# A two-layer decoder on one core: the result table's additions bound late in the last expert, pick matrices written by ScalarE, the table zeroed during attention, router bias and second tile reordered

## The chip, the cores and the metric

The kernel runs on one core of one Trainium2 chip. The metric is the device time of one execution in microseconds (us), as the median of several runs. Engines are named as in the profile: PE (TensorE matmul), PEld (its weight load), DVE (VectorE), ACT (ScalarE), POOL (GpSimd), SP (SyncE, which here only issues DMAs).

## The reference

A decoder of two layers on 256 tokens of width 1024, with 16 learned rows put in front (272 rows in all). Cut to what the change touches:

```python
for i in range(2):
    if i == 0: mix = rglru_block(h, ...)          # gated linear recurrence
    else:      mix = gla_block(h, ...)            # gated linear attention, 4 heads, chunks of 64
    h = layer_norm(ALPHA * h + mix, g, b)
    if i == 0: ff = swiglu(h, w_in, w_out)        # dense, width 3584
    else:      ff = moe_swiglu(h, ...)
    h = layer_norm(ALPHA * h + ff, g, b)

def moe_swiglu(h, router, w_in, w_out):           # 8 experts, 2 of them for each token
    logits = h @ router
    top_w, top_idx = softmax(top_k(logits, 2))
    y = 0
    for e in range(8):
        y = y + gate[:, e] * (silu(h @ w_in[e].gate) * (h @ w_in[e].up)) @ w_out[e]
    return y
```

## The kernel before

**Products and weights.** Every fp32 product is made of three fast ones: `mm3` (L271 to L275) multiplies the high part of a weight with the low part of the data, the low part with the high, and high with high. So each weight piece of 128x1024 has to be split before PE may use it: SP loads raw weights (L97), ACT casts a piece to its high part `whi` (L127), DVE subtracts to get the low part `wlo` (L137). Loads, casts and subtractions run ahead of PE by a few pieces.

**The mixture of experts.** The second half of the run goes through 8 experts of 7 stages each, 56 stages in all. A stage takes 12 weight pieces: 8 for the products `pg` and `pu` (tile xe of an expert's gathered tokens times the gate and up matrices), 4 for the product `y` back to width 1024. Between them ACT and DVE make `hb` = silu(pg) * pu (L1329, L1330), PE transposes it (`pt`), and ACT and DVE split that into `hh` and `hl` (L268, L269). The 56 `hb` rows mark the stages in what follows.

**Odd jobs.** All other work of this phase (slots of the experts, gathers, the table) is put into a queue `side`, whose `step` takes out some entries at each weight piece; an entry `lambda: None` is a blank that only lets time pass. The queue decides where the jobs stand in the program. A scheduler then sets the order of instructions on each engine from that program; `behind([x], f)` forbids that it places what f emits ahead of instruction x on the same engine. The part between attention and experts (from L1067) is in a section where the written order stands as it is.

**The result table.** Each of the first seven experts writes its result rows into a table `yd` in DRAM by an indirect DMA from POOL (`scatter`, L1371); rows that no expert writes must read as zero, so `clear` (L1272 to L1276) fills the table ahead of the first scatter. In the last expert `fetch_back` (L1282, POOL) reads the table back into two tiles `back`, and `add_back` (L1293, L1295) adds their four 128x1024 blocks on DVE to the residual `acc`. `split_acc` (L1446 on ACT, L1447 on DVE) splits the sum for a last matmul that adds it to the eighth expert's result.

**Slots.** For each expert, DVE writes selection matrices `sel` (L934) from the positions, PE multiplies them into `gs` (L1230), and DVE copies that to `slot_of` (L1232). `spread_pick` (L1199, POOL) makes four 128x512 matrices `pick`, which copy a row of a small table to all partitions by a matmul (`spread`).

**Router and second tile.** `router_sums` and `router_bias` (L707 to L712) give the bias of the router logits, from DVE's sums `rbs` by one matmul `rtb`. The 256 tokens are two tiles of 128. For each, `project` multiplies the attention result (`go`, `go11b`), `x3_add` adds it to the residual (L957), `x3_turn` transposes it on PE (`x3T`, L970), `logits` makes `lg`, `choose` finds the two experts (L1007 to L1013, `mask`), `rank` counts (L1020), `place` writes `pos` and `sel`. `x3_low` on POOL (L995) splits the normalised tile.

Of the kernel before, what the change touches and what calls it, by code (L numbers as in the profile page):

```python
# [11 lines left out]
F32 = mybir.dt.float32  # L12
# [57 lines left out]
class Weights:  # L70
# [62 lines left out]
    def lower(self, i, src, hi, lw):  # L133

        u, c, n = self.pieces[i]
        low = self.nc.gpsimd if i in self.aside else self.low
        low.tensor_sub(lw[:, :n], src, hi[:, :n])  # L137
        if c + n == self.units[u][1]:
            del self.raws[u]
            place = self.place.pop(u)  # L140
            if place[1] in self.retired:
                self.retired.pop(place[1])()
            else:
                self.free.append(place)
            self.load()
# [40 lines left out]
def trunk_kernel(ctx: ExitStack, tc: tile.TileContext, xT_d, rgp_d, lnT_d, rgin_d, rgg_d, rgout_d,  # L186
# [46 lines left out]

    const = ctx.enter_context(tc.tile_pool(name="const", bufs=1))
    ps = ctx.enter_context(tc.tile_pool(name="ps", bufs=8, space=PSUM))

    def bank(name):
        return ps.tile([P, 512], F32, tag="ps", name=name)
# [398 lines left out]
    wu = gp.tile([P, 512], F32, tag="vm", name="wu", bufs=1)  # L637
    nc.sync.dma_start(wu, wup_d)
    cm = gp.tile([P, P], F32, name="cm")
    cmask = gp.tile([P, P], U32, name="cmask")  # L640
    nc.gpsimd.affine_select(out=cm, in_=ones, pattern=[[1, P]], compare_op=ALU.is_ge, fill=0.0, base=0,
                            channel_multiplier=-1)
# [108 lines left out]

    side.drain()
    vm = gp.tile([P, D], F32, tag="vm", name="vm", bufs=1)
    side.put([lambda: None] * 36 + [router_sums] + [lambda: None] * 12 + [router_bias])
    for e in range(KD):
        pp = bank(f"vT{e}")
        for k in range(KD):
# [86 lines left out]
    def split_out(e):  # L844
        split(oh[:, e:e + 2], ol[:, e:e + 2], gr[:, e:e + 2])
# [25 lines left out]
    split_out(0)  # L871
    split_out(2)
    normalize(2)
    side.put([lambda: gate_out(4), lambda: gate_out(6), lambda: split_out(4), lambda: split_out(6)])
    pgo = [[bank(f"go{i}{q}") for q in range(2)] for i in range(2)]

    halves = [(slice(0, 256), pgo[1][1][:, :256]), (slice(256, 512), bank("go11b")[:, :256])]
# [40 lines left out]
    sels = {}  # L918
    late = ctx.enter_context(tc.tile_pool(name="late", bufs=1, reuse_waits="tile"))
    W.widen([(late, "late0"), (late, "late1"), (late, "late2"), (late, "xeC")])  # L920
    dram = ctx.enter_context(tc.tile_pool(name="dram", bufs=1, space=bass.MemoryType.DRAM))
    x3d = dram.tile([NX, D], F32, name="x3d")
    yd = dram.tile([2 * NX + P, D], F32, name="yd")
    gb = ctx.enter_context(tc.tile_pool(name="rows", bufs=1, reuse_waits="tile"))
    x3T = [gb.tile([P, 2, NX], F32, tag="xg", name=f"x3T{k2}", bufs=4) for k2 in range(4)]

# [140 lines left out]
    with tc.manual_schedule(engines={mybir.EngineType.PE, mybir.EngineType.DVE, mybir.EngineType.Activation}):  # L1067
        project((4, 5, 6, 7), ws, 0, 0)
        x3_add(0, 0)
        x3_stats(0, 0)  # L1070
        project((4, 5, 6, 7), ws, 0, 1)
        x3_turn(0, (0, 1))
        x3_add(0, 1)
        x3_stats(0, 1)
        project((4, 5), ws, 1, 0)
        x3_scale(0)
        x3_turn(0, (2, 3))
        logits(0, (0, 1))
        project((6,), ws, 1, 0)
        for q in range(2):  # L1080
            x3_norm(0, q)
        logits(0, (2, 3))
        project((7,), ws, 1, 0)
        choose(0)
        for q in range(2):
            x3_high(0, q)
            x3_low(0, q, nc.gpsimd)
        x3_add(1, 0)
        for k2 in range(2):
            x3_stats(1, k2)  # L1090
        project((4,), ws, 1, 1)
        project((5,), ws, 1, 1, halves[:1])
        x3_turn(1, (0, 1))
        project((6, 7), ws, 1, 1, halves[:1])
        pr = rank(0)
        x3_add(1, 1, halves[:1])
        W.later = []
        W.split_until(W.n_split + 1)
        place(0, pr)
        x3_stats(1, 2)  # L1100
        project((5,), ws, 1, 1, halves[1:])
        logits(1, (0, 1))
        x3_turn(1, (2,))
        project((6, 7), ws, 1, 1, halves[1:])
        x3_add(1, 1, halves[1:])
        W.split_until(W.n_split + 1)
        res.close()
        m2 = ctx.enter_context(tc.tile_pool(name="moe2", bufs=1, reuse_waits="tile"))
        W.widen([(m2, "xeB")])
        rows_of(0)  # L1110
        xgp[0] = bank("xg00")
        gather_part(xgp[0], 0, 0, 0)
        x3_turn(1, (3,))
        x3_stats(1, 3)
        x3_scale(1)
        logits(1, (2,))
        xgp[1] = bank("xg01")
        gather_part(xgp[1], 1, 0, 0)
        logits(1, (3,))
        for k2 in (2, 3):  # L1120
            xgp[k2] = bank(f"xg0{k2}")
            gather_part(xgp[k2], k2, 0, 0)
        choose(1)
        keep_warm(7)
        pr = rank(1)
        keep_warm(4)
        for q in range(2):
            x3_norm(1, q)
            x3_high(1, q)
        place(1, pr)  # L1130
        for q in range(2):
            x3_low(1, q, nc.vector)
        for k2s in ((0, 1), (2, 3)):
            for s in range(2):
                for k2 in k2s:
                    gather_part(xgp[k2], k2, 0, 1, (s,))
        first_rows(0, 0)
        lower(1)
        first_rows(1, 0)
        lower(1)  # L1140
        W.split_until(W.n_split + 1)
        first_rows(2, 0)
        lower(1)
        W.split_until(W.n_split + 1)
        first_rows(3, 0)
        lower(1)
        W.later = None
# [38 lines left out]

    picks, rows_hl = {}, []

    def spread_split():

        rows_hl.append(const.tile([P, 256], F32R, tag="onetri", name="rows_hl", bufs=1))
        nc.scalar.copy(rows_hl[0], rows)
        for at in (slice(32, 40), slice(96, 104)):
            nc.vector.tensor_sub(rows_hl[0][at], rows[at], rows_hl[0][at])

    def spread_pick(n, c):
        picks[n, c] = gb.tile([P, 4, P], F32R, tag="xg", name=f"pick{n}{c}", bufs=4)
        high, low = (ident[:, p0:p0 + 4, None].broadcast_to([P, 4, P]) for p0 in (64 * n + 4 * c, 64 * n + 4 * c + 32))
        nc.gpsimd.tensor_add(picks[n, c], high, low)  # L1199

    def spread(n, c, s):

# [65 lines left out]
            nc.tensor.transpose(pt[:, k * P:(k + 1) * P], x3r[e][:, (4 * h + k) * P:(4 * h + k + 1) * P], ident)  # L1268
        split(*(t[:, 4 * h:4 * h + 4].rearrange("p k t -> p (k t)") for t in xe[e]), pt)

    def clear():

        zero = late.tile([P, D], F32, tag="yrow", name="zero", bufs=1)
        nc.gpsimd.memset(zero, 0.0)
        for a in range(2 * NX // P):
            nc.gpsimd.dma_start(yd[a * P:(a + 1) * P], zero)  # L1276

    def store_x3():
        nc.gpsimd.dma_start(x3d.rearrange("(i p) d -> p i d", p=P), acc)

# [23 lines left out]
    def rows_1():  # L1304
        side.put([lambda: rows_of(1)] + [lambda k2=k2: split_rows(1, k2) for k2 in range(4)]
                 + [spread_split, lambda: behind(chosen, gate_values)]
                 + [lambda: [slots(e) for e in range(2)]])
        for e in range(2, NE, 2):
            side.put([lambda e=e: [pair(e)] + [select(g, i) for g in (e, e + 1) for i in range(2)],
                      lambda e=e: [slots(g) for g in (e, e + 1)]])  # L1310
        side.put([addresses, clear] + [lambda c=c: spread_pick(0, c) for c in range(2)]
                 + [lambda c=c, s=s, i=i: residual(c, s, i) for c in range(2) for s in range(2) for i in range(2)]
                 + [store_x3, lambda: None, lambda: fetch(2)])

# [143 lines left out]
    for n in range(NJ + 1):  # L1458
# [4 lines left out]
        if n > 0:  # L1463
            e, j = (n - 1) // JM, (n - 1) % JM
            if n == NJ:
                side.drain()
            stage_out(n - 1)
            if n == RB:
                W.retire("xeB", rows_1)
            if n == 5 * JM:  # L1470
                for tag in ("xeC", "late1", "late2"):
                    W.retire(tag, lambda: None)
            if j == 3 and 1 <= e < NE - 1:
                side.put([lambda e=e, h=h: turn(e + 1, h) for h in range(2)])
                if e < NE - 2:
                    side.put([lambda e=e: fetch(e + 2)])
            if e == NE - 1 and j == 0:
                lng[0] = m2.tile([P, 2, D], F32, tag="xeA", name="lng", bufs=1)
                side.put([last_slots] + [lambda c=c: spread_pick(1, c) for c in range(2)] + [lambda: None] * 4)
                side.put([lambda c=c, s=s: nc.scalar.copy(lng[0][:, c, s * 512:(s + 1) * 512], spread(1, c, s))  # L1480
                          for c in range(2) for s in range(2)])
                side.put([fetch_back] + [lambda: None] * 8)
                side.put([lambda k=k, i=i: add_back(k, i) for k in range(2) for i in range(2)])
                side.put([lambda i=i, s=s: split_acc(i, s) for s in range(2) for i in range(2)])
            if j == JM - 1 and e < NE - 1:
                while not placed:
                    side.items.popleft()()
                scatter(e)
# [163 lines left out]
```

## Time and profile before

| what | value |
|---|---|
| median of 3 runs | 1537.59 us (1536.28 to 1541.04) |
| profiled execution, own time | 1538.53 us |
| its span, first to last instruction | 1536.8 us |
| mean granted TensorE clock | 0.991 |
| PE busy | 1496.2 us (97%) |
| DVE busy | 1267.0 us (82%) |
| ACT busy | 1057.8 us (69%) |
| POOL busy | 125.6 us (8%) |

The span is what the trace covers; 1.7 us of the profiled execution's time lie outside it. The profiled execution took 0.94 us more than the median. The granted clock is TensorE's, as a share of full speed, and a busy share is an average over the whole span, so it says nothing of a single stage.

### The profile page before, as it was taken

What the parts mean: (1) busy time and instruction counts of PE and PEld (TensorE: products, weight loads), DVE (VectorE), ACT (ScalarE), POOL (GpSimd) and SP (SyncE); (2) the same over time, 40 slices, a digit from 0 to 9 for tenths busy, and PEclk for the clock granted to TensorE, in tenths of its full rate; (3) what the DMA queues carried; (4) which work ended last, traced back from release to release, by engine and by line L of the source; (5) the groups of instructions that cost most, each with busy time, mean ns of one, the idle gap of its engine ahead of it and who ended that gap; (6) DMA issues with size and microseconds to landing.
All of it is one profiled execution on the core that took longest, in us unless ns stands there. A gap on an engine that the chain in (4) does not pass through costs nothing.

```text
span 1536.8 us, 22261 instructions
## 1 busy us (share of the span) xinstructions
PE 1496.2 (97%) x8377; PEld 1305.5 (85%) x8377; DVE 1267.0 (82%) x1487; ACT 1057.8 (69%) x1364; POOL 125.6 (8%) x158
## 2 busy tenths in 40 slices
PE   8989999999999999999999999999999999997996
PEld 8989999999998878788888888888888888886884
DVE  7699755555876699899998889889899898896996
ACT  6866544444774598677887777677777786785774
POOL 5443000011100000200000000000000000000001
PEclk9999999999999999999999999999999999999998
DMA  9536544445452589899999999999998999998872
GB/s 369 182 134 220 192 172 171 144 172 187 165 189 86 220 314 391 307 341 423 400 371 369 360 380 387 364 391 383 359 390 309 368 372 389 377 361 341 308 269 104
DMA packets 68963, 450.65 MB, mean 293 GB/s; under 512 B 8144, under 2 KB 8432, under 8 KB 20720
## 3 DMA queue, kind: packets, MB, share of 16 engines
q1 hardware_dynamic: 65584, 437.10, 75.5%
q0 software_dynamic: 3264, 12.06, 2.0%
q8 instruction: 67, 1.10, 0.3%
q14 instruction: 48, 0.39, 0.1%
HBM read 441.26 MB, written 7.86 MB: 292 GB/s over the span
## 4 chain that ended last, share of the span: by engine, by line
PE 88%; DVE 6%; ACT 2%; issue 2%; DMA 1%; POOL 1%; SPq 0%; DVEq 0%; POOLq 0%; ACTq 0%
PE y L274 7%; PE y L275 7%; PE y L273 7%; PE pg L273 7%; PE pg L274 6%; PE pu L273 6%; PE pg L275 6%; PE pu L275 6%; PE pu L274 6%; DVE wlo L137 2%; PE fg L274 2%; PE fo L273 2%; PE fo L275 2%; PE fu L273 2%; PE fg L275 2%
## 5 line engine op out<-in xcount | busy, mean ns | idle before, releaser
L137 DVE TENSOR_TENSOR wlo<-raw,whi 128x1024 fp32r<-128x1024 f32 (+1 forms) x839 | 981.7, 1216 | 129.9 <-ACT whi L127 122.7
L127 ACT CAST whi<-raw 128x1024 fp32r<-128x1024 f32 (+1 forms) x841 | 835.1, 1037 | 169.6 <-PE fu L275 43.5
L274 PE MATMUL y<-wlo,hh 128*128 128x512 f32 x448 | 177.1, 395 | 9.5 <-DVE wlo L137 9.5
L273 PE MATMUL pg<-whi,xe 128*128 128x512 f32 x448 | 178.9, 399 | 0.7 <-DVE xe L1052 0.7
L274 PE MATMUL pg<-wlo,xe 128*128 128x512 f32 x448 | 179.1, 400 | 0.0
L275 PE MATMUL y<-whi,hh 128*128 128x512 f32 x448 | 177.0, 395 | 0.0
L273 PE MATMUL pu<-whi,xe 128*128 128x512 f32 x448 | 176.1, 393 | 0.0
L275 PE MATMUL pg<-whi,xe 128*128 128x512 f32 x448 | 175.9, 393 | 0.0
L275 PE MATMUL pu<-whi,xe 128*128 128x512 f32 x448 | 175.8, 392 | 0.0
L274 PE MATMUL pu<-wlo,xe 128*128 128x512 f32 x448 | 175.6, 392 | 0.0
L273 PE MATMUL y<-whi,hl 128*128 128x512 f32 x448 | 152.5, 396 | 0.0
L1329 ACT ACTIVATE hb<-pg 128x512 f32<-128x512 f32 x56 | 33.4, 596 | 135.0 <-PE pg L275 135.0
L274 PEld LDWEIGHTS y<-wlo,hh 128*128 128x128 f32 x448 | 85.4, 191 | 28.9 <-DVE wlo L137 10.2
L275 PEld LDWEIGHTS y<-whi,hh 128*128 128x128 f32 x448 | 85.1, 190 | 19.0
L273 PEld LDWEIGHTS y<-whi,hl 128*128 128x128 f32 x448 | 85.1, 190 | 18.4
L275 PEld LDWEIGHTS pu<-whi,xe 128*128 128x128 f32 x448 | 84.3, 188 | 18.9
L274 PEld LDWEIGHTS pu<-wlo,xe 128*128 128x128 f32 x448 | 84.3, 188 | 18.7
L273 PEld LDWEIGHTS pu<-whi,xe 128*128 128x128 f32 x448 | 84.3, 188 | 18.0
L273 PEld LDWEIGHTS pg<-whi,xe 128*128 128x128 f32 x448 | 84.4, 188 | 17.7 <-DVE xe L1052 0.9
L275 PEld LDWEIGHTS pg<-whi,xe 128*128 128x128 f32 x448 | 84.4, 189 | 16.7
L274 PEld LDWEIGHTS pg<-wlo,xe 128*128 128x128 f32 x448 | 84.5, 189 | 16.3 <-DVE wlo L137 0.3
L1330 DVE TENSOR_TENSOR hb<-hb,pu 128x512 f32<-128x512 f32 x56 | 38.3, 684 | 49.9 <-ACT hb L1329 48.3
(444 smaller groups left out, 2630.9 us busy)
## 6 DMA issues: line engine op xcount, KB each, us to landing
raw<-min SPq DMA_DIRECT2D x216, 1024.0 KB, 7.1
raw<-mout SPq DMA_DIRECT2D x106, 1024.0 KB, 7.3
raw<-fin SPq DMA_DIRECT2D x28, 1024.0 KB, 4.7
raw<-fout SPq DMA_DIRECT2D x16, 896.0 KB, 4.3
raw<-vr SPq DMA_DIRECT2D x8, 1024.0 KB, 4.5
raw<-min SPq DMA_DIRECT2D x16, 512.0 KB, 4.8
raw<-rgin SPq DMA_DIRECT2D x7, 1024.0 KB, 11.3
raw<-rgout SPq DMA_DIRECT2D x8, 704.0 KB, 3.9
```

Of the source, the lines that this page charges most:

```text
L127: self.high[i] = nc.scalar.copy(hi[:, :n], src).ins
L137: low.tensor_sub(lw[:, :n], src, hi[:, :n])
L273: nc.tensor.matmul(out_ap, w[1], xr[0], start=start, stop=False)
L274: nc.tensor.matmul(out_ap, w[0], xr[1], start=False, stop=False)
L275: nc.tensor.matmul(out_ap, w[0], xr[0], start=False, stop=stop)
L1329: behind(W.coming(n, 2), lambda: nc.scalar.activation(hb, pg, AF.Silu))
L1330: nc.vector.tensor_mul(hb, hb, pu)
```

## The change

Four edits. (1) `add_back` is bound behind the last weight subtraction that was emitted (`W.last_low`), after 5 blanks in place of 8, with a blank behind each of the four. (2) `pick` is written by ACT as a copy of a small tile `row_of`, which one small POOL addition makes ahead of time; before, POOL added two broadcast parts of the identity. (3) The table is zeroed at the start of attention from a 128x256 zero tile, whose row each DMA reads four times (512 rows of 1 KB); `clear` goes, and for the experts 2, 4 and 6 a blank stands between `select` and `slots`. (4) `router_bias` leaves the loop over `vT` with its 12 blanks and is put behind `split_out(6)`; in the written section, the addition of the second tile's first half (`x3_add(1, 0)`) stands ahead of `choose(0)`, and the `project` calls of its second half stand ahead of `x3_turn(1, (0, 1))` and of the logits.

```diff
@@ lower
-        low.tensor_sub(lw[:, :n], src, hi[:, :n])
+        self.last_low = low.tensor_sub(lw[:, :n], src, hi[:, :n]).ins
@@ start of attention
     cm = gp.tile([P, P], F32, name="cm")
+    zero = gp.tile([P, 256], F32, name="zero")
+    nc.gpsimd.memset(zero, 0.0)
+    for a in range(2 * NX // P):
+        nc.gpsimd.dma_start(yd[a * P:(a + 1) * P].rearrange("p (b c) -> p b c", b=4),
+                            zero[:, None, :].broadcast_to([P, 4, 256]))
@@ loop over vT
-    side.put([lambda: None] * 36 + [router_sums] + [lambda: None] * 12 + [router_bias])
+    side.put([lambda: None] * 36 + [router_sums])
@@
-    side.put([lambda: gate_out(4), lambda: gate_out(6), lambda: split_out(4), lambda: split_out(6)])
+    side.put([lambda: gate_out(4), lambda: gate_out(6), lambda: split_out(4), lambda: split_out(6),
+              router_bias])
@@ second tile
         project((7,), ws, 1, 0)
+        x3_add(1, 0)
         choose(0)
         for q in range(2):
             x3_high(0, q)
             x3_low(0, q, nc.gpsimd)
-        x3_add(1, 0)
         for k2 in range(2):
             x3_stats(1, k2)
         project((4,), ws, 1, 1)
-        project((5,), ws, 1, 1, halves[:1])
+        project((5, 6, 7), ws, 1, 1, halves[:1])
         x3_turn(1, (0, 1))
-        project((6, 7), ws, 1, 1, halves[:1])
         pr = rank(0)
...
-        project((5,), ws, 1, 1, halves[1:])
+        project((5, 6), ws, 1, 1, halves[1:])
+        x3_turn(1, (2,))
         logits(1, (0, 1))
-        x3_turn(1, (2,))
-        project((6, 7), ws, 1, 1, halves[1:])
+        project((7,), ws, 1, 1, halves[1:])
@@ picks
+    row_of = small("row_of", [P, 2, 8])
+    at_rows = ident[:, :].rearrange("p (n a k) -> p n a k", n=2, a=2)
+    nc.gpsimd.tensor_add(row_of, at_rows[:, :, 0, :8], at_rows[:, :, 1, :8])
...
-        high, low = (ident[:, p0:p0 + 4, None].broadcast_to([P, 4, P]) for p0 in (64 * n + 4 * c, 64 * n + 4 * c + 32))
-        nc.gpsimd.tensor_add(picks[n, c], high, low)
+        nc.scalar.copy(picks[n, c], row_of[:, n, 4 * c:4 * c + 4, None].broadcast_to([P, 4, P]))
@@ table
-    def clear():
-
-        zero = late.tile([P, D], F32, tag="yrow", name="zero", bufs=1)
-        nc.gpsimd.memset(zero, 0.0)
-        for a in range(2 * NX // P):
-            nc.gpsimd.dma_start(yd[a * P:(a + 1) * P], zero)
@@ first expert
-                      lambda e=e: [slots(g) for g in (e, e + 1)]])
-        side.put([addresses, clear] + [lambda c=c: spread_pick(0, c) for c in range(2)]
+                      lambda: None, lambda e=e: [slots(g) for g in (e, e + 1)]])
+        side.put([addresses] + [lambda c=c: spread_pick(0, c) for c in range(2)]
@@ last expert
-                side.put([fetch_back] + [lambda: None] * 8)
-                side.put([lambda k=k, i=i: add_back(k, i) for k in range(2) for i in range(2)])
+                side.put([fetch_back] + [lambda: None] * 5)
+                for k in range(2):
+                    for i in range(2):
+                        side.put([lambda k=k, i=i: behind([W.last_low], lambda: add_back(k, i)), lambda: None])
```

**DVE in the last expert.** In the order of before, the first addition of the table (L1293, out `acc`) stands two subtractions behind an `hl` and two ahead of the 51st `hb`, the second right behind that `hb`:

```order
L269 TENSOR_TENSOR hl_13850<-pt_13844,hh_13849 128x512
L137 TENSOR_TENSOR wlo_13835<-raw_13605,whi_13834 128x1024
L137 TENSOR_TENSOR wlo_13854<-raw_13605,whi_13853 128x1024
L1293 SCALAR_TENSOR_TENSOR acc<-acc,back_14142 128x1024
L137 TENSOR_TENSOR wlo_13866<-raw_13630,whi_13865 128x1024
L137 TENSOR_TENSOR wlo_13876<-raw_13630,whi_13875 128x1024
L1330 TENSOR_TENSOR hb_13909<-hb_13909,pu_13811 128x512
L1293 SCALAR_TENSOR_TENSOR acc<-acc,back_14142 128x1024
```

In the changed kernel the place between `hl` and the 51st `hb` holds subtractions only; the four additions (L1295 and L1297 there) stand behind the 53rd `hb`, and the first of them is one subtraction behind it:

```order
L1332 TENSOR_TENSOR hb_14236<-hb_14236,pu_14133 128x512
L137 TENSOR_TENSOR wlo_14214<-raw_13952,whi_14213 128x1024
L1295 SCALAR_TENSOR_TENSOR acc<-acc,back_14144 128x1024
L137 TENSOR_TENSOR wlo_14225<-raw_13952,whi_14224 128x1024
L137 TENSOR_TENSOR wlo_14240<-raw_13986,whi_14239 128x1024
```

So the first addition moved two stages on. The second stands six subtractions behind the first, and the two L1297 rows around the next `hl`; two of the four `acc_l` subtractions of `split_acc` come ahead of the 54th `hb`, two behind it. Between the 53rd and the 54th `hb` DVE has 14 subtractions in the changed kernel, between the 54th and the 55th 12.

**PE and DVE in the first expert.** On PE, before, the second group of `gs` (L1230) stands between two of the 12 weight pieces of a stage, six products each:

```order
L274 MATMUL pu_6992<-wlo_7025,xe_6179 128x512
L275 MATMUL pu_6992<-whi_7024,xe_6179 128x512
L1230 MATMUL gs_7122<-per_slot,sel_7107 128x4 x2
L1230 MATMUL gs_7126<-per_slot,sel_7107 128x4
L273 MATMUL pg_6991<-whi_7047,xe_6179 128x512
L1230 MATMUL gs_7126<-per_slot,sel_7107 128x4
L274 MATMUL pg_6991<-wlo_7048,xe_6179 128x512
L275 MATMUL pg_6991<-whi_7047,xe_6179 128x512
```

In the changed kernel it (L1239) stands one whole piece later, behind the products of `whi_7055` and `wlo_7056`:

```order
L277 MATMUL pg_6999<-whi_7055,xe_6185 128x512
L275 MATMUL pu_7000<-whi_7055,xe_6185 128x512
L276 MATMUL pu_7000<-wlo_7056,xe_6185 128x512
L277 MATMUL pu_7000<-whi_7055,xe_6185 128x512
L1239 MATMUL gs_7142<-per_slot,sel_7115 128x4 x2
L1239 MATMUL gs_7146<-per_slot,sel_7115 128x4 x2
L275 MATMUL y_6517<-whi_7085,hl_7052 128x512
```

On DVE, the `sel` that this `gs` reads stands before one subtraction behind `hl` and small copies:

```order
L269 TENSOR_TENSOR hl_7044<-pt_7038,hh_7043 128x512
L1170 TENSOR_REDUCE cnt<-count 128x1
L137 TENSOR_TENSOR wlo_7096<-raw_6717,whi_7095 128x1024
L1194 TENSOR_TENSOR rows_hl<-rows,rows_hl 8x256 x2
L1171 CAST cnti<-cnt 128x1
L1232 COPY slot_of<-gs_7087 128x4
L1232 COPY slot_of<-gs_7091 128x4
L934 TENSOR_SCALAR sel_7107<-slot,pos 128x128 x4
L137 TENSOR_TENSOR wlo_7113<-raw_6748,whi_7112 128x1024
L1232 COPY slot_of<-gs_7122 128x4
```

In the changed kernel it (L941) stands behind the same number of subtractions, and the copy of its result (`slot_of`, L1241) one subtraction further on:

```order
L271 TENSOR_TENSOR hl_7052<-pt_7046,hh_7051 128x512
L1204 TENSOR_TENSOR rows_hl<-rows,rows_hl 8x256 x2
L1176 TENSOR_REDUCE cnt<-count 128x1
L1241 COPY slot_of<-gs_7095 128x4
L1177 CAST cnti<-cnt 128x1
L1241 COPY slot_of<-gs_7099 128x4
L137 TENSOR_TENSOR wlo_7104<-raw_6725,whi_7103 128x1024
L941 TENSOR_SCALAR sel_7115<-slot,pos 128x128 x4
L137 TENSOR_TENSOR wlo_7121<-raw_6756,whi_7120 128x1024
L137 TENSOR_TENSOR wlo_7131<-raw_6756,whi_7130 128x1024
L1241 COPY slot_of<-gs_7142 128x4
```

The four `pick` rows, on POOL before, stand on ACT in the changed kernel, each with one or two `whi` casts between it and the next.

**PE at the second tile.** Before, the transposes of the second tile's first half (L970, in `acc`) stand ahead of six products `go` of its second half, and `rank` behind these:

```order
L275 MATMUL go_5877<-whi_5916,xh 128x256
L970 MATMUL x3T_6128<-ident,acc 128x128 x4
L273 MATMUL go_5877<-whi_5937,xl 128x256
L274 MATMUL go_5877<-wlo_5938,xh 128x256
L275 MATMUL go_5877<-whi_5937,xh 128x256
L273 MATMUL go_5877<-whi_5956,xl 128x256
L274 MATMUL go_5877<-wlo_5957,xh 128x256
L275 MATMUL go_5877<-whi_5956,xh 128x256
L1020 MATMUL rank_6141<-mask,onetri 128x8
```

In the changed kernel the six products (two pieces, three products each) come first, and then the transposes and `rank` (L977, L1027) one right behind the other:

```order
L275 MATMUL go_5883<-whi_5946,xl 128x256
L276 MATMUL go_5883<-wlo_5947,xh 128x256
L277 MATMUL go_5883<-whi_5946,xh 128x256
L275 MATMUL go_5883<-whi_5965,xl 128x256
L276 MATMUL go_5883<-wlo_5966,xh 128x256
L277 MATMUL go_5883<-whi_5965,xh 128x256
L977 MATMUL x3T_6140<-ident,acc 128x128 x4
L1027 MATMUL rank_6147<-mask,onetri 128x8
```

**DVE at the second tile.** The addition of that half (L957, out `acc`, in `go`) stands before behind the six steps that choose the experts of the first tile:

```order
L982 SCALAR_TENSOR_TENSOR rtx<-rtb,nmr 128x8
L1007 SCALAR_TENSOR_TENSOR lgt<-lg_6089,rsd,rtx 128x8
L1009 MAX top<-lgt 128x8
L1010 MAX_INDEX idx<-top,lgt 128x8
L1011 CAST idf<-idx 128x8
L1012 TENSOR_SCALAR o_6000<-iota_95,idf 128x8
L1013 SCALAR_TENSOR_TENSOR mask<-iota_95,idf,o_6000 128x8
L957 TENSOR_TENSOR acc<-acc,go_5876 128x512
```

In the changed kernel it (L964) stands ahead of these six, right behind `rtx`:

```order
L989 SCALAR_TENSOR_TENSOR rtx<-rtb,nmr 128x8
L964 TENSOR_TENSOR acc<-acc,go_5882 128x512
L1014 SCALAR_TENSOR_TENSOR lgt<-lg_6095,rsd,rtx 128x8
L1016 MAX top<-lgt 128x8
L1017 MAX_INDEX idx<-top,lgt 128x8
L1018 CAST idf<-idx 128x8
L1019 TENSOR_SCALAR o_6009<-iota_98,idf 128x8
L1020 SCALAR_TENSOR_TENSOR mask<-iota_98,idf,o_6009 128x8
```

## Rows read from the trace of the kernel before

**Rows 1.** Waits of PE: instruction, releaser: us in total, times, longest us.

```profile
PE y L274 <- DVE wlo L137: 9.5, 1, 9.5
...
PE x3T L970 <- DVE acc L957: 2.2, 1, 2.2
...
PE rtb L711 <- DVE rbs L707: 1.6, 1, 1.6
```

**Rows 2.** Timeline of DVE, last expert: start us, us, instruction, xcount [idle before <-releaser].

```profile
1403.44 2.35 DVE L137 TENSOR_TENSOR wlo<-raw,whi 128x1024 fp32r<-128x1024 f32 x2
1416.02 1.23 DVE L1293 SCALAR_TENSOR_TENSOR acc<-acc,back 128x1024 f32<-128x1024 f32 x1 [10.24 <-DMA back<-yd]
```

**Rows 3.** Timeline of POOL, last expert.

```profile
1407.98 1.51 POOL L1287 DMA_DIRECT2D back<-yd  x2 [7.63 <-DMA yd<-yrow,dest_u]
```

**Rows 4.** Timeline of PE, last expert.

```profile
1405.82 0.39 PE L273 MATMUL pu<-whi,xe 128*128 128x512 f32 x1
...
1408.34 0.62 PE L273 MATMUL y<-whi,hl 128*128 128x512 f32 x2
1418.44 0.80 PE L274 MATMUL y<-wlo,hh 128*128 128x512 f32 x1 [9.48 <-DVE wlo L137]
...
1424.56 0.40 PE L274 MATMUL y<-wlo,hh 128*128 128x512 f32 x1
```

**Rows 5.** Three stretches: us, busy time (x) of PE, PEld, DVE, ACT, POOL, PEclk, DMA share, GB/s.

```profile
402.00:413.00 11.00, 11.00 (x91) 11.00 (x90) 11.00 (x19) 8.84 (x18) 1.57 (x12) 1.00 0.32 107
525.00:530.00 5.00, 2.81 (x26) 2.66 (x25) 4.11 (x11) 1.59 (x3) 1.40 (x2) 1.00 0.42 170
1420.00:1425.00 5.00, 5.00 (x14) 3.89 (x13) 5.00 (x6) 2.09 (x2) 0.00 (x0) 0.55 0.77 234
```

**Rows 6.** Timeline of ACT, one undisturbed stage from hb to hb.

```profile
1391.14 0.60 ACT L1329 ACTIVATE hb<-pg 128x512 f32<-128x512 f32 x1 [3.98 <-PE pg L275]
...
1408.08 0.60 ACT L1329 ACTIVATE hb<-pg 128x512 f32<-128x512 f32 x1 [2.70 <-PE pg L275]
```

**Rows 7.** Timeline of DVE, the stage ahead of that.

```profile
1375.77 9.17 DVE L137 TENSOR_TENSOR wlo<-raw,whi 128x1024 fp32r<-128x1024 f32 x8 [0.25 <-ACT whi L127]
...
1391.77 0.69 DVE L1330 TENSOR_TENSOR hb<-hb,pu 128x512 f32<-128x512 f32 x1 [1.69 <-ACT hb L1329]
```

**Rows 8.** Timeline of POOL, first expert.

```profile
618.52 3.06 POOL L1199 TENSOR_TENSOR pick<-ident 128x512 fp32r<-128x512 f32 x2 [92.12 <-PE y L275]
```

**Rows 9.** Timeline of DVE, first expert.

```profile
617.96 0.76 DVE L269 TENSOR_TENSOR xe<-xgs,xe 128x256 fp32r<-128x256 f32 x2
618.63 2.06 DVE L137 TENSOR_TENSOR wlo<-raw,whi 128x1024 fp32r<-128x1024 f32 x1
620.62 1.25 DVE L269 TENSOR_TENSOR xe<-xgs,xe 128x256 fp32r<-128x256 f32 x1
...
631.36 1.35 DVE L934 TENSOR_SCALAR sel<-slot,pos 128x128 fp32r<-128x128 f32 x4
...
635.74 0.86 DVE L934 TENSOR_SCALAR sel<-slot,pos 128x128 fp32r<-128x128 f32 x4
```

**Rows 10.** Timeline of PE, first expert.

```profile
632.41 1.22 PE L1230 MATMUL gs<-per_slot,sel 128*128 128x4 f32 x6 [2.52 <-DVE sel L934]
...
639.55 0.39 PE L274 MATMUL y<-wlo,hh 128*128 128x512 f32 x1
```

**Rows 11.** Timeline of DVE, second tile.

```profile
524.06 1.15 DVE L1011 CAST idf<-idx 128x8 f32<-128x8 uint32 x1
...
526.61 0.68 DVE L957 TENSOR_TENSOR acc<-acc,go 128x512 f32<-128x512 f32 x1
```

**Rows 12.** POOL's table zeroing, grouped by form: busy us, mean ns | idle before.

```profile
L1276 POOL DMA_DIRECT2D yd<-zero x4 | 2.4, 625 | 0.3 <-POOL zero L1274 0.3
```

**Rows 13.** Timeline of DVE at the start of attention.

```profile
413.14 0.22 DVE L644 CAST cmask<-cm 128x128 uint32<-128x128 f32 x1
```

**Rows 14.** Timeline of POOL at the start of attention.

```profile
402.11 0.14 POOL L643 MEMSET cm<- 64x64 f32 x1
```

More of the change, by code (lines that the diff above doesn't have):

```diff
@@ L235, in trunk_kernel @@
     ps = ctx.enter_context(tc.tile_pool(name="ps", bufs=8, space=PSUM))
+    dram = ctx.enter_context(tc.tile_pool(name="dram", bufs=1, space=bass.MemoryType.DRAM))
+    yd = dram.tile([2 * NX + P, D], F32, name="yd")
     def bank(name):
@@ L920, in trunk_kernel @@
     W.widen([(late, "late0"), (late, "late1"), (late, "late2"), (late, "xeC")])
-    dram = ctx.enter_context(tc.tile_pool(name="dram", bufs=1, space=bass.MemoryType.DRAM))
     x3d = dram.tile([NX, D], F32, name="x3d")
-    yd = dram.tile([2 * NX + P, D], F32, name="yd")
     gb = ctx.enter_context(tc.tile_pool(name="rows", bufs=1, reuse_waits="tile"))
```

## Prediction

> **What bounds the kernel.** I read the busy shares first (the table above: PE 97%), so only time in which PE waits or runs at a lower clock can be saved. The second view is the list of PE's waits. Four waits matter for this change: one of 9.5 us for a weight's low part, one of 2.2 us for the residual of the second tile, one of 1.6 us for the sums `rbs` [rows 1], and one of 2.5 us for `sel` [rows 10]. Each happens once, so each has a place, and I then read the timelines there.
>
> *Last expert.* DVE ends its subtractions and then stands 10.24 us in front of the first addition of the table, until the table's DMA has landed [rows 2]. That DMA was issued at 1407.98, after 7.63 us in which POOL waited for the last scatter [rows 3], and landed 8.0 us later (1416.02). The subtractions behind the addition on DVE's queue are what PE waits for: PE stops for 9.48 us [rows 4]. It also pays afterwards. Eleven products start between 1405.82 and 1408.34, one each 0.229 us. From 1418.44 to 1424.56 there are 14, which take 6.12 us in place of 14 x 0.229 = 3.21 [rows 4]. The granted clock of 1420 to 1425 is 0.55, about the lower of the two levels (1.2 of 2.4 GHz) [rows 5]. So this place costs 9.48 + 2.91 = **12.4 us**.
>
> *An undisturbed stage* is 16.94 us from ACT's `hb` to ACT's `hb` [rows 6]. A subtraction takes (9.17 - 0.08) / 8 = 1.137 us, and DVE stands 1.69 us before its `hb` [rows 7]. With `hl` and `hb` (0.60 each from start to start, in the row 0.69) DVE has 12 x 1.137 + 1.2 = 14.84 us of work a stage, which leaves 2.1 us.
>
> *First expert.* POOL writes `pick` matrices from 618.52 on [rows 8], and DVE's two-input instructions beside them are longer: a subtraction takes 2.06 where an undisturbed row has 1.22 (2.35 for two in [rows 2], whose ends overlap), and an `xe` 1.25 where two took 0.76 just before [rows 9], some 0.42 for one. Four DVE rows are stretched so, by about 0.83 each, 3.3 us together (the first two are shown). The four `sel` then take 1.35 beside POOL's table zeroing, elsewhere 0.86 [rows 9]. PE stands 2.52 us, and then takes 7.14 us from 632.41 to 639.55 for 13 products and 8 small `gs` [rows 10], which would be 13 x 0.229 plus some 8 x 0.1 = 3.8 us at full clock. So this place costs 2.52 + 3.3 = **5.8 us**.
>
> **The change, part by part.**
>
> *Additions of the table.* They go behind the 53rd `hb`. Counted from the 1408.08 of [rows 6], which belongs to the 51st, two stages of 16.94 put that at 1442, 26 us behind the landing at 1416.02. The other edits move both ends alike. So the wait for the table goes, with its slow products: -12.4. What is late next is DVE itself. From the 53rd to the 55th `hb` it gets four additions (1.23 long in [rows 2], as long as a subtraction, so 1.14 from start to start) and four `acc_l` (0.60 each, by the two-input 128x512 row of [rows 7]): 4.56 + 2.40 = 6.96 us, against 2 x 2.1 = 4.2 us that two stages leave. Behind each addition on DVE's queue stand the next subtractions, and PE waits for those. So some 2.8 us come back as several waits of PE of at most one addition (1.14) each. Around the wait of 2.2 us the granted clock stayed at 1.00 (525 to 530) [rows 5]; behind the waits of 2.5 and 9.5 us the products were slow [rows 4, 10]. So I take no slow clock here. The bounds: 0, if the pieces in hand hold more than the count says, and 2.8 + 2.9 = 5.7, if one drop of the clock follows. A drop also gives DVE 2.9 us, so there is no second. I take **+2.8**.
>
> *Picks.* The four POOL additions leave, so the 3.3 us of stretched DVE rows go. ACT gets four 128x512 copies, at about 0.60 us each by its 128x512 row [rows 6], 2.4 us. ACT stands 2.7 to 4.0 us for PE ahead of an `hb` [rows 6], and that hides them; without this cover the casts would be up to 2.4 us late. `row_of` is one small addition far ahead of its use.
>
> *First `gs`.* PE now reaches it one weight piece later (6 x 0.229 = 1.37 us), the `sel` loses its company (-0.49), DVE is 3.3 us earlier: 5.2 us against a wait of 2.52. That is 2.6 us to spare, just more than the 2.4 that the picks could cost ACT and so DVE. I take the whole **-5.8**.
>
> *Zeroing at the start of attention.* Four issues of 512 rows stand on POOL ahead of the corner memset of `cm`, which ran at 402.11 [rows 14]; its reader on DVE comes at 413.14 [rows 13]. So POOL has 10.9 us. An issue of 128 rows took 0.625 us [rows 12]: four take between 2.5 us (by issue) and 10.0 us (by rows). Both ends are under 10.9, hence **0**, and I lean to the lower end. If the cover were gone, DVE would stand by the excess. Here the Trainium skill speaks against the change: SBUF — State Buffer, section "SBUF: two separate sides", says that a DMA issued from GpSimd cannot get its descriptors written while DVE runs in a two-port mode. Its section "A bandwidth-pool intuition that's wrong (but worth ruling out)" gives about 620 ns alone and 3100 ns beside such an operation. By that, an estimate, the four take 12.4 us, the cast is 1.5 us late, and the sum below would be 17.0 in place of 18.5. The mean of 0.625 is of issues with DVE busy beside them, though what ran then may not have been such an operation.
>
> *Router bias.* PE's wait for `rbs` goes [rows 1]; at its new place the sums have long been made, and the matmul is two short rows as before: **-1.6**.
>
> *Second tile.* DVE's first sum of that tile ran at 526.61, behind the choice of the first tile's experts [rows 11], and PE stood 2.2 us for it [rows 1]. Now it stands ahead of the choice, and six half products (about 0.7 us) fill PE meanwhile. But `rank` follows the transposes at once and needs `mask`, which comes 0.7 us later on DVE for the sum (0.68 in its row) that now stands ahead of it. The choice still has its slow cast (1.15) [rows 11]. PE will stand some 0.7 us there: I take 2.2 - 0.7 = **-1.5**, with bounds 0 and -2.2.
>
> **Sum.** -12.4 + 2.8 - 5.8 + 0 - 1.6 - 1.5 = **-18.5 us**. The profiled execution took 1538.53, which gives 1520.0; it was 0.94 above the median, so against 1537.59 I predict **1519.1**.
>
> **Rivals.**
> 1. *DVE is late in the last two stages and the clock falls once.* For it: 6.96 against 4.2 us. Against: single waits below 1.2 us. +2.9: **1522.0**.
> 2. *The first expert's wait only moves,* to the copy of `slot_of` or the next reader of that group, because the cast and the subtraction behind it are late by the picks. For it: ACT gets 2.4 us of work. Against: 2.6 us to spare. It gives back up to 5.8: **1524.9**.
> 3. *No new wait in the last expert.* For it: in the kernel before the same additions and `acc_l` stood in about two stages, with no other row for them among PE's waits. Against: PE was slower there by 2.9 us, and DVE caught up. **1516.3**.
> 4. *POOL cannot issue while DVE is busy.* DVE is busy for all of 402 to 413 [rows 5]. If the issues wait for a pause, they get it only when DVE stops at the cast of `cmask` and waits for POOL: four issues of 0.625, 2.5 us, of which PE sees at most all: **1521.6**. The page named above states such a mechanism.
> 5. *The other side.* The small waits of stages 53 to 55 take the clock to its lower level and keep it there. Each product then costs 0.437 (6.12 / 14) in place of 0.229. To be slower by 0.3%, this must eat 18.5 + 4.6 = 23.1 us, 111 products, over one and a half stages: from there on, **1542.2** and more. Against: at that pace a piece lasts 2.6 us on PE and 1.14 on DVE, so DVE is ahead at once, and in both places of before the clock came back within 14 products.
> 6. *The change doesn't do what it says:* the additions still wait for the table. It would have to land over 26 us later than seen. With 12.4 left and the 2.8 not paid: about **1528.7**.
>
> **Chances.** Forecast 0.58, rival 1 0.12, rival 2 0.10, rival 3 0.11, rival 4 0.04, rival 5 0.02, rival 6 0.03. The unknown second tile adds 1.5 up and 0.7 down, so the range runs from rival 3 less 0.7 and one for the spread between executions (1514.5) to rival 2 plus 1.5, and a bit of rival 4 (1527.5). 0.3%, 4.6 us, is about what a measurement of this kernel can tell from no change. All cases but rival 5 end below 1533: faster 0.94, same 0.03 (two or three of the gains missing at once), slower 0.03.
>
> **What would show it.** Right: no DVE row that waits for the table; the additions at 1.2 us behind the 53rd `hb`; waits of PE for `wlo` in stages 53 to 55 of below 1.2 us, about 2.8 together, at a granted clock of 1.00. No wait of PE for `sel` at the first `gs`, subtractions of 1.22 all through the first expert, `pick` rows on ACT of about 0.6. `rtb` without a wait; one wait of about 0.7 us at `rank` in the second tile. `cmask` not waiting for POOL. Wrong: a stretch with a clock near 0.5 in the last expert, a PE wait in the sixth stage, or zero issues that last until 413.

## The result and the profile after

The changed kernel takes 1519.18 us (median of 4, 1518.28 to 1519.64), the kernel before 1539.32 beside it (4 runs, 1536.28 to 1541.52). The ratio is 0.9870, with a 95% interval of 0.9849 to 0.9891: faster by 20 us, and at the predicted 1519.1 (the forecast started from the earlier median of 1537.59 and took off 18.5). The two traces show that this sum came out by luck, through two errors of opposite sign. First some of what PE waits for in the changed kernel (us in total, times, longest):

```profile
PE y L672 <- ACT zr L687: 5.3, 1, 5.3
...
PE rank L1027 <- DVE mask L1020: 0.8, 1, 0.8
...
PE y L276 <- DVE wlo L137: 0.6, 1, 0.6
...
PE pg L276 <- DVE wlo L137: 0.4, 1, 0.4
```

The four waits of [rows 1, 10] are gone. A new one of 5.3 us stands in attention, at a place where the kernel before had none. The same landmarks in both traces say where the time went (the start of `identr`, a cast on POOL just ahead of attention; the starts of `hb` on ACT; the span's end):

| stretch | before, us | after, us | difference |
|---|---|---|---|
| start to `identr` | 399.93 | 399.33 | -0.6 |
| `identr` to the 1st `hb` | 152.56 | 156.58 | +4.0 |
| 1st to 9th `hb` | 138.80 | 131.80 | -7.0 |
| 9th to 51st `hb` | 716.79 | 711.60 | -5.2 |
| 51st to 53rd `hb` | 47.86 | 35.49 | -12.4 |
| 53rd `hb` to the end | 80.86 | 82.50 | +1.6 |

Between the 9th and the 51st `hb` the edits change only the blanks ahead of the slots of experts 2, 4 and 6, and still 5.2 us are gained there, 0.10 to 0.15 in nearly every stage. ACT's timeline of the 50th and 51st `hb` shows it:

```profile
1382.52 0.60 ACT L1331 ACTIVATE hb<-pg 128x512 f32<-128x512 f32 x1 [3.93 <-PE pg L277]
...
1399.31 0.60 ACT L1331 ACTIVATE hb<-pg 128x512 f32<-128x512 f32 x1 [2.61 <-PE pg L277]
```

16.79 us, where [rows 6] have 16.94, at a granted clock of 1.00 in both, and with DVE's and ACT's instructions as long as before. PE itself is faster, by 0.7% over the 42 stages.

*The loss in attention.* POOL's timeline there:

```profile
401.37 0.94 POOL L646 DMA_DIRECT2D yd<-zero  x1
405.81 0.74 POOL L646 DMA_DIRECT2D yd<-zero  x1 [3.50 <-issue]
409.47 0.71 POOL L646 DMA_DIRECT2D yd<-zero  x1 [2.93 <-issue]
416.32 0.72 POOL L646 DMA_DIRECT2D yd<-zero  x1 [6.13 <-issue]
416.95 0.25 POOL L651 MEMSET cm<- 64x64 f32 x1
```

An issue is 0.7 to 0.9 us long, near the lower estimate of 0.625, but 2.9 to 6.1 us of waiting stand between them. The first three landed 4.1, 3.4 and 6.5 us after their start, at 405.49, 409.17 and 416.01, and each next issue starts 0.30 to 0.32 us after that landing. The corner of `cm`, written at 402.11 before [rows 14], is written at 416.95. DVE comes to it at 412.6 and stands:

```profile
412.12 0.50 DVE L398 SCALAR_TENSOR_TENSOR xl<-x,lnT,xh 128x272 fp32r<-128x272 f32 x1
417.23 1.46 DVE L652 CAST cmask<-cm 128x128 uint32<-128x128 f32 x1 [4.62 <-POOL cm L651]
```

Behind the cast on DVE's queue are the sums for `zr`, so PE stands for 5.3 us, and the clock falls (busy time of PE, PEld, DVE, ACT, POOL, then the granted clock, DMA share, GB/s):

```profile
415.00:420.00 5.00, 0.32 (x3) 0.11 (x1) 2.71 (x8) 0.52 (x1) 2.29 (x12) 0.73 0.33 116
420.00:425.00 5.00, 4.33 (x18) 3.82 (x18) 5.00 (x14) 3.35 (x6) 0.00 (x0) 0.59 0.50 157
```

*The other places.* DVE in the last expert, first expert and second tile of the changed kernel, three timelines that answer to [rows 2, 9, 11]:

```profile
1436.37 1.23 DVE L137 TENSOR_TENSOR wlo<-raw,whi 128x1024 fp32r<-128x1024 f32 x1 [0.25 <-ACT whi L127]
1437.51 1.22 DVE L1295 SCALAR_TENSOR_TENSOR acc<-acc,back 128x1024 f32<-128x1024 f32 x1
```

```profile
621.55 1.22 DVE L137 TENSOR_TENSOR wlo<-raw,whi 128x1024 fp32r<-128x1024 f32 x1
622.69 0.42 DVE L271 TENSOR_TENSOR xe<-xgs,xe 128x256 fp32r<-128x256 f32 x1
...
631.13 0.87 DVE L941 TENSOR_SCALAR sel<-slot,pos 128x128 fp32r<-128x128 f32 x4
```

```profile
528.85 0.69 DVE L964 TENSOR_TENSOR acc<-acc,go 128x512 f32<-128x512 f32 x1 [2.10 <-PE go L277]
...
530.18 1.03 DVE L1018 CAST idf<-idx 128x8 f32<-128x8 uint32 x1
```

The addition waits for nothing. With POOL's picks gone, a subtraction beside the `xe` takes 1.22 and an `xe` 0.42. The sum of the second tile stands ahead of the choice and waits only for its product. The choice, with its slow cast (1.03), now ends behind that sum, and `rank` waits 0.8 us for it.

### The profile page after: what moved, and what is told of

It is laid out like the page before. It is cut to its first block, busy times and chain, and to the rows that moved or that the text cites. A ratio compares the mean times of both kernels' runs of the same rounds, so it can differ in the third digit from the quotient of the medians.

```text
span 1517.3 us, 22245 instructions
## 1 busy us (share of the span) xinstructions
PE 1485.7 (98%) x8377; PEld 1301.7 (86%) x8377; DVE 1261.6 (83%) x1487; ACT 1059.1 (70%) x1368; POOL 118.8 (8%) x155
## 4 chain that ended last, share of the span: by engine, by line
PE 90%; DVE 4%; ACT 2%; issue 2%; POOL 1%; DMA 0%; SPq 0%; DVEq 0%; ACTq 0%; POOLq 0%
PE pg L276 7%; PE pg L277 7%; PE pg L275 7%; PE pu L276 7%; PE pu L277 7%; PE pu L275 7%; PE y L275 6%; PE y L276 6%; PE y L277 6%; PE fg L276 2%; PE fu L275 2%; PE fg L277 2%; PE fo L275 2%; PE fo L277 2%; PE fo L276 2%
```

## The experiments

Two questions: why the zeroing held POOL, and where PE's pace comes from. Then each other edit alone. Kernels of one group ran beside the kernel before on one chip (medians 1540.19, 1537.35 and 1539.04 us in the three groups).

**The kernel before again** (no edit).

> The kernel before, unchanged. In the profiled execution of before a product took 0.2288 us from start to start in the undisturbed stages of the experts (a stage 16.94 us), in that of the changed kernel 0.2270 (16.80), which makes about 6 us over the eight experts that no edit explains. Theory 1, the pace is a thing of the single execution or of the chip it ran on: here it may be either, and all kernels of this call have nearly one pace. Theory 2, the pace belongs to the program (its layout in memory): here 16.94 again, and 16.80 in the kernels made from the changed one.

1540.81 us (one run), and the median stage is 16.94 again, while the three kernels of this group that are made from the changed one have 16.81. So the pace goes with the program and not with the execution, nor with the chip: two later kernels that leave the tiles at their old place have 16.94 on two other chips. Two things differed from the profiled execution of before. Fewer slow products stood behind the wait for `sel` (77.14 us from the 5th to the 9th `hb`, 78.72 before). And the 2.2 us wait of the second tile was followed by slow products. PE's row of that wait, and the next stretch:

```profile
528.25 0.66 PE L970 MATMUL x3T<-ident,acc 128*128 128x128 f32 x4 [2.22 <-DVE acc L957]
```

```profile
530.00:535.00 5.00, 5.00 (x25) 5.00 (x25) 1.71 (x6) 1.85 (x3) 0.00 (x0) 0.50 0.01 2
```

**The zeroing behind the memsets.**

```diff
-    zero = gp.tile([P, 256], F32, name="zero")      # and its memset and four DMAs
     cmask = ...
     for t in scb + kta[0] + kta[1] + ktb:
         nc.gpsimd.memset(t, 0.0)
+    zero = gp.tile([P, 256], F32, name="zero")      # and its memset and four DMAs
```

> The changed kernel, with the zero tile and its four DMAs put behind the memsets of cm, scb, kta and ktb on POOL. Theory 1, an issue of 512 rows waits on POOL until the DMA before it has landed: the four issues keep their spacing of 3.7 to 7 us and end near 419, the cast of cmask waits for nothing, PE's wait of 5.3 us for zr and the slow products behind it are gone, 1511 us (1519.2 less about 8). Theory 2, DVE's instructions block the issues: the same rows, but the spacing follows DVE's pauses, and 1511 as well. Theory 3, the wait at zr is not from the zeroing: PE's wait stays, 1519.

1512.14 us (4 runs, 1511.51 to 1513.98), ratio to before 0.9819 (0.9797 to 0.9841). POOL writes the corner early, and the fourth issue comes 12.2 us after the first (405.52), where the changed kernel has 15.0:

```profile
403.48 0.14 POOL L646 MEMSET cm<- 64x64 f32 x1
...
409.37 0.74 POOL L665 DMA_DIRECT2D yd<-zero  x1 [2.90 <-issue]
413.21 0.71 POOL L665 DMA_DIRECT2D yd<-zero  x1 [3.10 <-issue]
417.73 0.72 POOL L665 DMA_DIRECT2D yd<-zero  x1 [3.81 <-issue]
```

The busy times from the first to the fourth issue (PE, PEld, DVE, ACT, POOL, then clock and DMA as above):

```profile
405.52:417.73 12.21, 12.21 (x99) 12.06 (x97) 12.21 (x28) 11.88 (x23) 2.40 (x3) 1.00 0.64 230
```

PE has no wait in this stretch. DVE is busy for all of it, and the issues go all the same, each 0.30 to 0.32 us after the landing of the one before (409.05, 412.90, 417.43). So theory 1 holds and theory 2 falls. The issues are nearly as slow as in the changed kernel; only what stood behind them on POOL made them cost. From `identr` to the 1st `hb` it takes 149.5 us in place of 156.58: the zeroing cost 7.1 us.

**The zeroing issued by SP** (`nc.sync.dma_start` in place of `nc.gpsimd.dma_start`).

> The changed kernel, with the four DMAs that zero the table issued by SP at the same place of the program. Theories 1 and 2: POOL is free, cmask waits for nothing, 1511 us, unless the weight loads behind them on SP's queue come late, which would show as a wait of PE for a low part in attention (up to 15 us of queue time). Theory 3: 1519.

1512.53 us (4 runs), ratio 0.9829 (0.9805 to 0.9852), 149.5 us for the same stretch, and no PE wait for a weight in attention.

**The zeroing in eight DMAs of 256 rows.**

```diff
-    for a in range(2 * NX // P):
-        nc.gpsimd.dma_start(yd[a * P:(a + 1) * P].rearrange("p (b c) -> p b c", b=4),
-                            zero[:, None, :].broadcast_to([P, 4, 256]))
+    for a in range(4 * NX // P):
+        nc.gpsimd.dma_start(yd[a * 64:(a + 1) * 64].rearrange("p (b c) -> p b c", b=4),
+                            zero[:64, None, :].broadcast_to([64, 4, 256]))
```

> The changed kernel, with the table zeroed at the same place by eight DMAs of 256 rows in place of four of 512. Theory 1, with room for some number of rows in flight: two issues (512 rows) go at once, or more if the room is between 512 and 1024, then each waits for a landing, the last issue near 414 to 416, cmask late by 2 to 4 us, 1517 to 1519. Theory 2, each issue waits for DVE: eight waits in place of four, cmask later than before, 1520 or more.

1511.50 us (one run). Both theories had expected cmask late; it was not:

```profile
400.84 2.10 POOL L646 DMA_DIRECT2D yd<-zero  x3
405.25 0.59 POOL L646 DMA_DIRECT2D yd<-zero  x1 [2.31 <-issue]
...
410.67 0.59 POOL L646 DMA_DIRECT2D yd<-zero  x1 [0.74 <-issue]
411.24 0.18 POOL L651 MEMSET cm<- 64x64 f32 x1
```

Three issues (768 rows) go one behind the other, and the fourth starts 0.32 us after the first has landed (404.93). Each of the last four starts 0.31 us after the landing of the issue three places ahead of it. So 768 rows are taken without a wait and 1024 are not; of issues of 512, only one at a time. It is not the bytes: each of the four issues of 128 rows in [rows 12] moves as many as an issue of 512 rows here (512 KB), and they went back to back. With smaller issues POOL is free 5.7 us earlier than in the changed kernel. The changed kernel speaks against DVE as the cause too: DVE stood idle from 412.6 to 417.2, and POOL went on waiting until 416.32.

**Only a tile of 64 bytes.** The four edits together add one small tile, `row_of`, 64 bytes a partition. By the compiler's list of addresses, which no trace shows, the tiles up to it lie at the same places in both kernels, and what follows lies 64 bytes higher. So `xe`, `hh` and `hl`, the 128x128 operands that PE loads (the expectation below calls them moving; the weights are the wide, moving ones), start 64 bytes past a multiple of 512 before and 128 past it after. `whi` and `wlo` start 128 past in both.

```diff
     picks, rows_hl = {}, []
+    nc.gpsimd.memset(small("pad", [P, 16]), 0.0)
```

> The kernel before with one more tile of 64 bytes a partition, in the place where the changed kernel has row_of, set to zero once and never read. Every later tile of that side (xe, hh, hl among them, which PE reads as moving operands) then starts 64 bytes on, at a multiple of 128 bytes, as in the changed kernel. Theory 1, the place of these tiles sets PE's pace: a product takes 0.2272 us in place of 0.2290, a stage 16.81 in place of 16.94, and the time is about 7 us under the kernel before, with all four waits of PE still there. Theory 2, the pace comes from another part of the change (the order of instructions, the table's place in DRAM): 0.2290, 16.94, no change.

ACT's `hb`, two of the stages:

```profile
1065.35 0.60 ACT L1330 ACTIVATE hb<-pg 128x512 f32<-128x512 f32 x1 [3.93 <-PE pg L275]
1082.17 0.60 ACT L1330 ACTIVATE hb<-pg 128x512 f32<-128x512 f32 x1 [3.93 <-PE pg L275]
```

16.82 us: a tile that nobody reads gives the pace of the changed kernel. From the 1st to the 56th `hb` it takes 947.35 us, the kernel before again 954.44. The medians differ by less than the 7 us expected, 1533.56 (8 runs) to 1537.35, ratio 0.9970 (0.9958 to 0.9983). Its runs have a mean granted clock of 0.988 to 0.990 where those of before have 0.989 to 0.992. Its trace shows one place: behind the 1.6 us wait for `rbs` the clock was 0.66 over the next 5 us, where the kernel before, run again, has 1.00, and from `identr` to the 1st `hb` it took 157.04 us against 155.42. Why the clock fell there is open.

**The changed kernel, 64 bytes on** (the same line in the changed kernel).

> The changed kernel with another such tile of 64 bytes, so that xe, hh and hl start 64 bytes off a multiple of 128 again. Theory 1: a stage takes 16.94, and the time is about 7 us over the changed kernel, 1526. Theory 2: 16.81, 1519.

1541.68 us (one run), further than either theory: all the gain is lost, with the waits of the changed kernel unchanged.

```profile
1072.99 0.60 ACT L1332 ACTIVATE hb<-pg 128x512 f32<-128x512 f32 x1 [4.08 <-PE pg L277]
1090.23 0.60 ACT L1332 ACTIVATE hb<-pg 128x512 f32<-128x512 f32 x1 [4.08 <-PE pg L277]
```

17.24 us a stage. So the remainder to 128 bytes does not decide (64 past 128 in this kernel as in that of before).

**Only the additions, late** (the diff's edits of `lower` and of the last expert).

> The kernel before with only the additions of the table bound late. The wait of 9.5 us and its 14 slow products go (12.4 us), and PE gets small waits in stages 53 to 55: by the prediction 2.8 us together, by the trace of the changed kernel 1.0. So 9.6 to 11.4 us under the kernel before. Were the gain of the last expert a matter of the other edits, it would be under 5.

1527.95 us (5 runs, 1525.75 to 1533.00), 9.4 under before and so just short of the 9.6 expected, ratio 0.9946 (0.9926 to 0.9966). Its PE waits for `wlo` are those of the changed kernel, 0.6 and 0.4. It shows a second thing. Its wait for `sel` in the first expert is as long as in [rows 10], but the clock stays up behind it:

```profile
633.15 0.80 PE L1230 MATMUL gs<-per_slot,sel 128*128 128x4 f32 x6 [2.53 <-DVE sel L934]
```

```profile
635.00:640.00 5.00, 5.00 (x23) 4.09 (x22) 5.00 (x9) 3.95 (x5) 0.68 (x2) 1.00 1.00 381
```

**Only the picks on ACT** (with a 64-byte tile beside `row_of`).

> The kernel before with only the pick matrices written by ACT, and 64 bytes more beside row_of, so that xe, hh and hl keep their place against 128 bytes. Theory 1, POOL's picks beside DVE made sel late: DVE is 3.3 us earlier, sel is in time or late by under 0.5 us, 5 to 6 us under the kernel before. Theory 2, the copies on ACT take it back, or the later gs was needed too: PE still waits 1 us or more at gs or at a low part of that stage, and the gain is under 3 us.

1548.81 us (4 runs), ratio 1.0072 (1.0047 to 1.0098): slower, by the pace, since the tiles now lie 192 past a multiple of 512 and a stage takes 17.24 (0.30 more in each of 56 stages is 16.8 us). The first expert itself is as theory 1 says: PE has no wait for `sel` and none for a low part there. From the 5th to the 9th `hb` it takes 73.82 us, less 4 x 0.30 for the pace 72.6, where the kernel before has 78.72 and, run again, 77.14, and the version with only the additions, whose clock stayed up, 75.50.

**Only router bias and second tile** (the diff's edits of these two).

> The kernel before with only the router bias moved and the second tile reordered, the tiles xe, hh and hl at their old place. By the prediction: no wait for rbs, a wait of about 0.7 us for mask in place of 2.2 for the residual, 3.1 us under the kernel before, the first hb of the experts about 3 us earlier counted from identr. Rival: the second tile only moves its wait (to rank or to the second choice), and only the 1.6 us of the router bias remain.

1532.91 us (10 runs) to 1539.04, ratio 0.9959 (0.9944 to 0.9973), so 4 to 9 us. In its profiled execution the stretch from `identr` to the 1st `hb` is 149.47 us, 3.1 under the 152.56 of before, as predicted, and of the waits that the edit was for one is left, shortened:

```profile
PE rank L1021 <- DVE mask L1014: 0.8, 1, 0.8
```

The rest of the gain is most likely the slow products behind the 2.2 us wait. Five traces here have that wait: in the profiled execution of before the clock of the next 5 us was 1.00, in the other four (the kernel before again, the pad, the additions, the picks) 0.55 to 0.68.

**Other places for the tiles.** The version with eight DMAs, with 128 and with 384 bytes more (`pad` of 32 and of 96 columns).

> The changed kernel with the zeroing in eight DMAs and 128 bytes more in front of xe, hh and hl, which then start 256 bytes past a multiple of 512 (64 before, 128 in the changed kernel, 192 in the two slow runs). Theory 1, the pace is best where the 128x128 operand that PE loads has the weight tile's remainder to 512, which is 128: slower than 0.2272 us a product, 1515 or more. Theory 2, only the remainder to 128 counts beside a smaller effect: 0.2272 or less, 1511 or less.

> As the run with 256, with 384 bytes more: xe, hh and hl start at a multiple of 512. Theory 1 (the weight tile's remainder): slower than 0.2272 us a product, 1515 or more. Theory 2 (the remainder to 128): 0.2272 or less, 1511 or less.

1532.22 and 1532.03 us (9 runs each), ratios 0.9961 (0.9947 to 0.9976) and 0.9957 (0.9941 to 0.9973): 20 us over the one run of the same kernel without the tile, at 17.23 us a stage in both. Of five places tried, 128 past a multiple of 512 gives 16.81, 64 gives 16.94, and 192, 256 and 0 give 17.23 to 17.24. Theory 2 falls. Theory 1 is not refuted; that equality with the weight's remainder decides was not tried by moving the weights.

**`xe` kept, `hh` and `hl` moved** (a 64-byte tile between `xe` and `hb`, so `hb` moves with them).

> The changed kernel with the zeroing in eight DMAs and 64 bytes more between xe and hb: xe stays at 128, hh and hl go to 192 past a multiple of 512. If the place of the loaded operand itself sets the pace, the products of y (from hh and hl) take 0.233 us and those of pg and pu (from xe) stay at 0.227; a stage takes about 16.95. If another tile's place does it (one written by ACT or DVE beside PE), both kinds change alike or neither does.

1520.37 us (one run), 16.96 us a stage. PE's timeline in one stage:

```profile
1059.70 0.63 PE L275 MATMUL y<-whi,hl 128*128 128x512 f32 x2
...
1063.89 0.39 PE L275 MATMUL pg<-whi,xe 128*128 128x512 f32 x1
...
1065.72 0.39 PE L275 MATMUL pg<-whi,xe 128*128 128x512 f32 x1
...
1068.44 0.39 PE L275 MATMUL pg<-whi,xe 128*128 128x512 f32 x1
```

18 products of `y` from 1059.70 to 1063.89 take 0.2328 us each; 12 of `pg` and `pu` from 1065.72 to 1068.44 take 0.2267. From the 13th to the 49th `hb`, the mean time from one such product to the next of its kind is 0.2334 and 0.2275, and in the version with eight DMAs alone, where all lie at 128, 0.2267 and 0.2276. So the place of the loaded operand sets the pace of its own products.

## Why the prediction was right, and where it was not

The time, the sign and the range held, the time by luck. By its own terms:

- *Last expert, -12.4:* 12.1 by the trace (12.4 from the 51st to the 53rd `hb`, less two stages of 0.13). Right.
- *DVE late in its place, +2.8:* +2.0 (1.6 from the 53rd `hb` on, plus 0.4 for the pace), of which 1.0 are listed as waits; the other 1.0 is open. Right in kind, a little too large. The clock stayed at full and no row waited for the table, so rivals 1, 5 and 6 fell, and rival 3 with the waits.
- *First expert, -5.8:* -6.0 (7.0 from the 1st to the 9th `hb`, less eight stages of 0.13). Right for these two executions. But the 3.3 us of slow products in it are not there in every execution, or not in full: from the 5th to the 9th `hb` the run with only the additions took 75.50 us and that with only router and tile 75.54, where before has 78.72. The wait of 2.5 us itself is in every trace that lacks the edit of the picks. Rival 2 fell.
- *Router bias and second tile, -3.1:* 3.1 in the trace of these two edits alone. The step "Around the wait of 2.2 us the granted clock stayed at 1.00" was true of one execution and false of the four others traced with that wait, so the gain over many runs is larger.
- *Zeroing, 0:* the step that failed, **+7.1** measured. "Four take between 2.5 us (by issue) and 10.0 us (by rows). Both ends are under 10.9" bounded the length of the issues, not the waiting between them. Measured from the first issue to the corner memset it is 15.6 us: each issue of 512 rows waited for the one before to land. The prediction's own sign of being wrong, zero issues that last until 413, came. Rival 4 had the place, but not the cause or the size (2.5 us). By the Trainium skill (SBUF — State Buffer, sections "SBUF: two separate sides" and "A bandwidth-pool intuition that's wrong (but worth ruling out)") the estimate was 12.4 us for the four. That is nearer than mine, but the reason it gives does not fit: POOL waited through 3.7 us in which DVE was idle (412.6 to 416.3), and with the zeroing behind the memsets four issues went out while DVE was busy all the time, each right behind a landing.
- *Not in the sum at all:* PE's pace, **-7** over the experts. `row_of` was costed as "one small addition far ahead of its use"; what counted was its 64 bytes.

The two errors, +7.1 and about -7, cancel to within the spread between executions. So the total was right by luck, and the account behind it was not complete. Undoing the one error without the other gives the fastest versions here: the changed kernel with the zeroing behind the memsets, 1512.14 us, or issued by SP, 1512.53; the one run with eight DMAs took 1511.50.

## What to carry to other kernels

Compare an undisturbed stage of both kernels before reading any wait: a uniform change of pace is in no list of waits, and an edit that adds a small tile moves every tile behind it. A DMA that is put on an engine's queue has to be costed to its last issue, with what stands behind it there; put it behind whatever others wait for, or on a queue that can spare the time, as SP's could here (no new wait of PE). What one execution shows of the clock behind a wait of 2 to 2.6 us is one draw; the wait itself repeats.

## What the hardware showed that was not expected

- 64 bytes in the place of the 128x128 operand that PE loads change one of the fast products (128x512, type fp32r) by up to 2.6%: a stage of 16.81 us (128 past a multiple of 512 bytes), 16.94 (64), 17.23 to 17.24 (0, 192, 256), at a granted clock of 1.00. Why is open.
- POOL took three DMA issues of 256 rows at once, and of issues of 512 rows only one. Each further one started 0.30 to 0.32 us after a landing: with 256 rows that of the third before it, with 512 that of the one before (waits of 2.9 to 6.1 us). Where between 768 and 1024 rows the limit lies was not tried.
- Behind a PE wait of 2.2 to 2.6 us, the granted clock of the next 5 us was 0.52 to 0.73 in some executions and 1.00 in others, at the same places of the same instructions (2.2 us: low in four of five traces; 2.5 to 2.6 us: in three of five). Behind the 1.6 us wait for `rbs` it was 0.66 in one trace and 1.00 in four; behind those of up to 0.8 us in the changed kernel it stayed at 1.00.
